# Attention's weight-by-value products: high and low halves in one 512-column product, with odd heads' values stored low half first

## The chip, the cores and the metric

The kernel runs on one core of a Trainium2 chip, as one launch. A core has five engines with instruction queues of their own: TensorE (PE; matrix products, its weight loads are shown as PEld), VectorE (DVE), ScalarE (ACT), GpSimd (POOL) and SyncE (SP, which here only issues transfers). The metric is device time in microseconds. Before the change the median of three runs is 2846.95 us (2845.26 to 2849.56).

## The reference

One decoder layer over 2048 tokens of 1024 features, in fp32: a token mixer (a depthwise convolution group beside a group of 8 attention heads of 64), cross attention into 256 memory tokens, and an MLP with squared ReLU, each with an RMS norm before and after. What matters here is the attention:

```
logits = einsum("bqhd,bkhd->bhqk", qb, kb) * scale
logits = logits + cum[:, :, q0:kl, None] - cum[:, :, None, :kl]   # forget-gate bias
p = softmax(where(mask, logits, NEG_INF))                         # causal
out = einsum("bhqk,bkhd->bqhd", p, vb)
```

## The kernel before

Features lie on partitions and tokens along the free axis; tokens are taken in 4 chunks of 512. TensorE multiplies `float32r` operands. To hold precision each fp32 operand is split into a high half (a ScalarE copy into `float32r`) and a low half (VectorE: the value minus its high half), and a product of two fp32 matrices is three products: high by high, high by low, low by high (`mm3`, lines 165 to 167).

**Attention's values.** `mix_in` projects 128 tokens by 4 heads at a time and stores for each head and token 128 numbers: its 64 high, then its 64 low halves (lines 365 to 370). So one 128x128 stationary tile holds both halves of V of one head for 128 keys: its output has 128 partitions, 64 from the high and 64 from the low half.

**Weight by value.** `values` (line 581) does it for one head and 256 queries (`QB`), in groups of two key tiles of 128. For each group TensorE transposes the softmax weights into the PSUM tile `pt` (line 595, three or four products of 128 columns), ScalarE and VectorE split `pt` into the two halves of `pp` (line 599), and, one group later, TensorE multiplies into the PSUM tile `o` (line 611): for each key tile one product of 256 columns by the high half of the weights and one by the low half, all added in the same 256 columns. The last key tile of a block meets only the second 128 queries, with products of 128 columns. When the block is done, `otmp` gathers the two partition halves of `o`: ScalarE copies one, VectorE adds the other (lines 617 and 618), and SP stores it to `datt`. `o` has one PSUM bank, `pp` two slots, and `otmp` shares the three slots of the tag `bs` with the diagonal bias `dg` (line 544), which GpSimd makes.

There are 64 such blocks: 8 heads, 4 chunks, 2 blocks of queries each. A block has 2, 4, ... 16 key tiles, by its place in the sequence.

**What sets the order.** A generator for the main stream (projections, then the MLP of an earlier chunk) and one for the side stream (attention, output projection, cross attention) are driven in step by the costs that they yield (`drive`); the convolution's taps are put between as background work for VectorE. The framework's scheduler then orders each engine's instructions by priorities counted in instructions (`ahead`, `steps`) and by when it holds them to be ready. From `attend(0)` on, the products of line 611 so stand between the main stream's `mm` products, in an order that is fixed before the launch.

Of the kernel before, what the change touches and what calls it, by code (L numbers as in the profile page):

```python
# [38 lines left out]
# Slots of the tile tags. Tiles of one tag are handed out in program order, so each stream of work  # L39
# (projections and MLP; attention and cross attention; convolution) has tags of its own.  # L40
BUFS = {
    "wr": 2, "wh": 2, "wl": 2, "xh": 1, "xl": 1,          # 4 KB: weights, raw and split
    "mk": 6, "bk": 7, "vk": 1,                            # 8 KB
    "mu": 5, "bu": 2, "bp": 2,                            # 4 KB
    "ms": 4, "bs": 3, "vs": 4,                         # 2 KB
    "row": 2,
    "mm": 2, "sc": 2, "pt": 2, "o": 1, "stat": 1,         # PSUM banks
# [3 lines left out]
# Chunk 0 takes also the slots that attention does not need then.  # L51
# [3 lines left out]
# The schedule: how far streams' instructions are put ahead of (h*), the work that they are given beside  # L55
# the main stream (r0, a1, m*), that of the convolution (a0, b1, bm), and what steps count for (y*).
# [4 lines left out]
class Engine:  # L61
    """An engine; pinned, it takes its instructions in program order."""
# [18 lines left out]
class Trunk:  # L81
# [13 lines left out]
    # ---------------------------------------------------------------- tiles  # L95
# [17 lines left out]
    # -------------------------------------------------------------- helpers  # L113
    @contextmanager
    def ahead(self, n):
        """Instructions put n places ahead of the others'."""
        n = 0 if Engine.pinned else n
        self.tc.cur_priority -= int(n)
        yield
        self.tc.cur_priority += int(n)  # L120
# [17 lines left out]
    def scaled_split(self, hi, lo, x, s):  # L138
        """(hi, lo) of x * s, s a constant or one value per partition."""
        self.a.activation(hi, x, AF.Copy, scale=s)  # L140
        self.v.scalar_tensor_tensor(
            out=lo, in0=x, scalar=s, in1=hi.bitcast(F32), op0=ALU.mult, op1=ALU.subtract)

    def weight(self, src, shape, into=None, g=MAIN):
        """One 4 KB per partition block of weights as float32r high and low parts."""
# [14 lines left out]
    def mm3(self, ps, lhs, rhs, first=True, last=True):  # L160
        """ps (+)= sum over k of lhsT.T @ rhs, each operand a (high, low) pair."""
# [15 lines left out]
    def token_mean(self, ss, mean):  # L177
        """Mean over the features of ss ([128, w], partial sums): PSUM [128, w / 128], tokens on partitions."""
# [6 lines left out]
    def token_rstd(self, ss, mean):  # L185
        """1 / sqrt(mean + eps) per token, as token_mean."""
# [6 lines left out]
    def spread(self, r):  # L193
        """Values per token, [128, n] with tokens on partitions -> PSUM [128, n * 128], the same on every partition."""
# [12 lines left out]
    def pair8(self, w, name, tags):  # L207
        """Two high and two low [128, 4, w] tiles, in the order h l h l of the tags."""
# [3 lines left out]
    # ------------------------------------------------------------ constants  # L212
# [51 lines left out]
    # ---------------------------------------------------- memory keys/values  # L264
# [13 lines left out]
    def normed(self, xs, g, w, stag, out=None, tags=None):  # L278
        """rms_norm of xs, two [128, 4, w] tiles, in place; with tags also split, as in halves."""
# [20 lines left out]
    def halves(self, out, xs, w, tags):  # L300
        """out: the float32r (high, low) tiles of xs, two [128, 4, w] tiles."""
# [34 lines left out]
    # ------------------------------------------------- token mixer, projection  # L336
    def mix_in(self, h, ht, late, after):
        """Input projection of half h; late brings its second chunk, after follows its first chunk's last use."""
# [16 lines left out]
        for b in range(2):  # L355
# [5 lines left out]
            for t in range(8):  # L361
# [3 lines left out]
                v = self.tile("ms", [P, 4, 2, DH], F32R, name="v")  # L365
                pv = ps[:, :256].rearrange("p (h d) -> p h d", d=DH)
                self.split(v[:, :, 0], v[:, :, 1], pv)
                self.store(
                    self.d_v[h][4 * b : 4 * b + 4, :, t].rearrange("h p d -> p h d"),
                    v.bitcast(F32).rearrange("p h l d -> p h (l d)"))  # L370
# [41 lines left out]
    def conv_push(self, c, t):  # L412
        """Background vector work: the depthwise convolution of channel tile t in chunk c, to DRAM."""
# [21 lines left out]
    def conv_norm(self, a, tag):  # L435
        """LayerNorm over the channels and swish of a ([128, 4, 512]), in place."""
# [22 lines left out]
    def gate(self, h, ht):  # L459
        """-cumsum(log_sigmoid(h @ w_f + b_forget)) of one half, to DRAM."""  # L460
# [31 lines left out]
    # ------------------------------------------------------ forgetting attention  # L492
    def attend(self, c):
        """Queries of chunk c against all keys up to them, head by head."""
# [86 lines left out]
    def values(self, c, hd, b, prow, v):  # L581
# [4 lines left out]
        o = self.ps("o")[:, :QB]  # L586
        prev = None
        for k0 in range(0, nk + 2, 2):
            cur = None
            if k0 < nk:  # L590
                # The last key tile meets only the second half of the queries.
# [9 lines left out]
            if prev is not None:  # L601
                g, pp = prev
                order = [(0, 0), (0, 1), (1, 0), (1, 1)]
                if g == nk - 2:
                    order = [(0, 0), (1, 0), (1, 1), (0, 1)] if g == 0 else order[2:] + order[:2]
                for n, (k, l) in enumerate(order):
                    if g + k == nk - 1:
                        out, rhs = o[:, P:], pp[:, l, QB : QB + P]
                    else:
                        out, rhs = o, pp[:, l, k * QB : (k + 1) * QB]  # L610
                    nc.tensor.matmul(out, v[:, g + k], rhs, start=g == 0 and n == 0, stop=g == nk - 2 and n == 3)  # L611
# [473 lines left out]
```

## Time and profile before

| | |
|---|---|
| time, median of 3 runs | 2846.95 us (2845.26 to 2849.56) |
| profiled execution: span from the first to the last instruction | 2843.6 us |
| median above that span (launch and end; the page has no other time) | 3.3 us |
| TensorE products busy | 2779.2 us, 98%, 14020 products |
| TensorE weight loads busy | 2310.6 us, 81% |
| VectorE busy | 1967.2 us, 69%, 3521 instructions |
| ScalarE busy | 1380.7 us, 49% |
| GpSimd busy | 206.5 us, 7% |
| products of line 611 | 1152 of the 14020 |

A product's busy time in the profile is its time from start to modelled end. Products are pipelined, so the next starts before that end: what a product costs in a stream is the distance from its start to the next one's start, its pitch. "Idle" of an engine is given with its releaser, the work that ended the wait.

### The profile page before, as it was taken

Reading aid. Unit: us, or ns where it says so; the run is one execution under the profiler, and the core shown is the slowest. Engines: PE = TensorE matmul, PEld = TensorE weight load, DVE = VectorE, ACT = ScalarE, POOL = GpSimd, SP = SyncE. Lnnn points to the kernel's source line nnn. Section 1 sums busy time; section 2 is a strip of 40 time slices with the busy share of each in tenths; the row PEclk is TensorE's granted clock in tenths of the full one; section 3 lists DMA queues with packets and bytes.
Section 4 is the critical chain, followed back from the end, with each engine's and each line's share of the span. In section 5 each row is a group of like instructions: output and inputs, shape, how many; then the busy total and the mean of one; then the engine's idle time right before and its main releaser. Section 6 shows DMA issues by size and latency. Waiting matters only on the chain.

```text
span 2843.6 us, 37412 instructions
## 1 busy us (share of the span) xinstructions
PE 2779.2 (98%) x14020; PEld 2310.6 (81%) x14020; DVE 1967.2 (69%) x3521; ACT 1380.7 (49%) x2164; POOL 206.5 (7%) x367
## 2 busy tenths in 40 slices
PE   7999999999999999999999999999999999999998
PEld 6889778888888887878888888788887888888887
DVE  7877896769787676788886645886665555743446
ACT  5323654345654445466554445665554445543332
POOL 0010300001110000012100001020100000000000
PEclk9999999999999999999999999999999999999999
DMA  5365744456544444455543435464524342343232
GB/s 168 117 217 170 174 128 163 141 164 200 154 137 132 124 136 145 149 151 175 138 142 119 146 108 166 129 197 129 155 94 128 126 145 93 130 144 97 96 97 81
DMA packets 141045, 398.32 MB, mean 140 GB/s; under 512 B 15248, under 2 KB 37904, under 8 KB 136000
## 3 DMA queue, kind: packets, MB, share of 16 engines
q1 hardware_dynamic: 99952, 262.40, 28.9%
q0 software_dynamic: 40912, 133.54, 16.4%
q8 instruction: 110, 1.80, 0.3%
q14 instruction: 71, 0.58, 0.1%
HBM read 330.68 MB, written 65.20 MB: 139 GB/s over the span
## 4 chain that ended last, share of the span: by engine, by line
PE 80%; issue 4%; DMA 4%; DVE 4%; ACT 2%; POOL 0%; SPq 0%; DVEq 0%; POOLq 0%; ACTq 0%
PE mm L165 18%; PE mm L166 18%; PE mm L167 18%; PE o L611 5%; PE sc L167 4%; PE sc L165 4%; PE sc L166 4%; PE pt L595 3%; PE sc L561 2%; PE sc L562 2%; DMA ks<-dk 1%; DVE acc L73 1%; DVE yacc L73 1%; DMA wr<-in_w_up_dram 1%; PE stat L182 1%
## 5 line engine op out<-in xcount | busy, mean ns | idle before, releaser
L73 ACT CAST wh<-wr 128x1024 fp32r<-128x1024 f32 x282 | 296.6, 1052 | 715.5 <-PE mm L166 634.1
L165 PE MATMUL mm<-h,wh 128*128 128x512 f32 x1504 | 597.6, 397 | 5.5 <-ACT h L73 2.6
L167 PE MATMUL mm<-h,wl 128*128 128x512 f32 x1504 | 596.9, 397 | 0.0
L166 PE MATMUL mm<-h,wh 128*128 128x512 f32 x1504 | 595.1, 396 | 1.7 <-DVE h L73 1.7
L73 DVE TENSOR_TENSOR wl<-wr,wh 128x1024 fp32r<-128x1024 f32 x282 | 345.5, 1225 | 277.2 <-ACT wh L73 276.0
L165 PE MATMUL mm<-hid,wh 128*128 128x512 f32 x992 | 395.3, 399 | 0.4 <-DVE yacc L73 0.4
L167 PE MATMUL mm<-hid,wl 128*128 128x512 f32 x992 | 392.8, 396 | 0.0
L166 PE MATMUL mm<-hid,wh 128*128 128x512 f32 x992 | 392.8, 396 | 0.0
L73 DVE SCALAR_TENSOR_TENSOR acc<-cu,convw,acc 128x512 f32<-128x512 f32 x480 | 356.9, 747 | 5.8
L165 PEld LDWEIGHTS mm<-h,wh 128*128 128x128 f32 x1504 | 283.9, 189 | 65.2 <-ACT h L73 2.9
L166 PEld LDWEIGHTS mm<-h,wh 128*128 128x128 f32 x1504 | 283.8, 189 | 60.1 <-DVE h L73 3.2
L167 PEld LDWEIGHTS mm<-h,wl 128*128 128x128 f32 x1504 | 283.6, 189 | 58.4
L73 DVE TENSOR_TENSOR yacc<-mm,yacc 128x512 f32<-128x512 f32 (+1 forms) x232 | 155.0, 669 | 160.3 <-PE mm L167 158.7
L73 DVE TENSOR_TENSOR pp<-pt,pp 128x512 fp32r<-128x512 f32 (+1 forms) x288 | 186.9, 656 | 68.0 <-ACT pp L73 66.6
L73 ACT CAST pp<-pt 128x512 fp32r<-128x512 f32 (+1 forms) x288 | 159.5, 560 | 124.6 <-PE pt L595 116.0
L165 PEld LDWEIGHTS mm<-hid,wh 128*128 128x128 f32 x992 | 186.3, 188 | 39.6 <-DVE yacc L73 1.5
L167 PEld LDWEIGHTS mm<-hid,wl 128*128 128x128 f32 x992 | 186.5, 188 | 38.5 <-issue 0.5
L166 PEld LDWEIGHTS mm<-hid,wh 128*128 128x128 f32 x992 | 186.6, 188 | 36.5 <-DVE hid L73 0.3
L595 PE MATMUL pt<-ident,prow 128*128 128x128 f32 x1088 | 199.3, 274 | 1.0 <-ACT prow L73 0.9
L73 ACT ACTIVATE prow<-prow,mx 128x128 f32<-128x128 f32 (+15 forms) x128 | 154.2, 1205 | 76.7 <-DVE mx L73 74.1
L73 DVE CUSTOM_DVE_ANT_0 prow<-sc,bias 128x512 f32<-128x512 f32 (+3 forms) x288 | 166.8, 596 | 34.3 <-PE sc L562 29.6
L611 PE MATMUL o<-pp,vv 128*128 128x256 f32 (+1 forms) x832 | 178.8, 299 | 8.6 <-DVE pp L73 7.9
(234 smaller groups left out, 4585.5 us busy)
## 6 DMA issues: line engine op xcount, KB each, us to landing
wr<-in_w_up_dram SPq DMA_DIRECT2D x128, 512.0 KB, 3.5
wr<-in_w_down_dram SPq DMA_DIRECT2D x128, 512.0 KB, 3.5
wr<-in_w_in_dram SPq DMA_DIRECT2D x32, 512.0 KB, 4.4
q<-dq POOLq DMA_DIRECT2D x64, 256.0 KB, 6.1
wr<-in_w_out_dram SPq DMA_DIRECT2D x32, 512.0 KB, 3.5
dx<-y SPq DMA_DIRECT2D x16, 1024.0 KB, 4.2
bias<-dnc POOLq DMA_DIRECT2D x32, 512.0 KB, 5.7
x<-in_x_dram POOLq DMA_DIRECT2D x12, 1024.0 KB, 5.9
```

The lines of the kernel that those rows point to most:

```text
L73: ins = op(*args, **kw)
L165: mm(ps, ah, bh, start=first and j == 0, stop=False)
L166: mm(ps, ah, bl, start=False, stop=False)
L167: mm(ps, al, bh, start=False, stop=last and j == n - 1)
L182: self.nc.tensor.matmul(ps[:, t : t + 1], ss[:, t * P : (t + 1) * P], mean, start=True, stop=True)
L561: nc.tensor.matmul(ps[:, :w], q[:, 0, qs], ks[:, k0 : k0 + w], start=True, stop=False)
L562: nc.tensor.matmul(ps[:, :w], q[:, 1, qs], ks[:, k0 : k0 + w], start=False, stop=True)
L595: nc.tensor.transpose(pt[:, at : at + P], prow[t][:, (k0 + k) * P : (k0 + k + 1) * P], self.ident)
L611: nc.tensor.matmul(out, v[:, g + k], rhs, start=g == 0 and n == 0, stop=g == nk - 2 and n == 3)
```

## The change

In `mix_in`, the tile `v` has four groups of 64 for each pair of heads: the even head's high and low, then the odd head's low and high. In `values`, one product takes both halves of the weights: its moving operand is two runs of 256 numbers, the high and the low half of `pp`, and its output is the whole bank of `o`, 512 columns. The stationary tile is the same. So the output has four quarters: (V high, V low) by (weights high, weights low). The last key tile takes two runs of 128. Three of the quarters are added at the end, V low by weights low is not taken: ScalarE copies the quarter from the other partitions, and VectorE adds two quarters from the head's own partitions, where the odd heads now have their high half too.

```diff
-                v = self.tile("ms", [P, 4, 2, DH], F32R, name="v")
-                pv = ps[:, :256].rearrange("p (h d) -> p h d", d=DH)
-                self.split(v[:, :, 0], v[:, :, 1], pv)
+                v = self.tile("ms", [P, 2, 4, DH], F32R, name="v")
+                pv = ps[:, :256].rearrange("p (g e d) -> p g e d", e=2, d=DH)
+                self.split(v[:, :, 0:4:3], v[:, :, 1:3], pv)
                 self.store(
                     self.d_v[h][4 * b : 4 * b + 4, :, t].rearrange("h p d -> p h d"),
-                    v.bitcast(F32).rearrange("p h l d -> p h (l d)"))
+                    v.bitcast(F32).rearrange("p g (e l) d -> p (g e) (l d)", e=2))
...
-        o = self.ps("o")[:, :QB]
+        o = self.ps("o").rearrange("p (l q) -> p l q", l=2)
...
-                order = [(0, 0), (0, 1), (1, 0), (1, 1)]
-                if g == nk - 2:
-                    order = [(0, 0), (1, 0), (1, 1), (0, 1)] if g == 0 else order[2:] + order[:2]
-                for n, (k, l) in enumerate(order):
-                    if g + k == nk - 1:
-                        out, rhs = o[:, P:], pp[:, l, QB : QB + P]
-                    else:
-                        out, rhs = o, pp[:, l, k * QB : (k + 1) * QB]
-                    nc.tensor.matmul(out, v[:, g + k], rhs, start=g == 0 and n == 0, stop=g == nk - 2 and n == 3)
+                every, late = slice(0, QB), slice(P, QB)
+                if g < nk - 2:
+                    order = [(0, every), (1, every)]
+                elif g > 0:
+                    order = [(1, late), (0, every)]
+                else:
+                    order = [(0, slice(0, P)), (0, late), (1, late)]
+                for n, (k, q) in enumerate(order):
+                    at = 0 if k == 0 else QB - q.start
+                    nc.tensor.matmul(o[:, :, q], v[:, g + k], pp[:, :, at + q.start : at + q.stop],
+                                     start=g == 0 and k == 0 and (n == 0 or nk == 2),
+                                     stop=g == nk - 2 and (n != 0 if g > 0 else n != 1))
...
-        self.a.copy(tmp[mine], o[other])
-        self.add(tmp[mine], o[mine], tmp[mine])
+        self.a.copy(tmp[mine], o[other, 0])
+        self.add(tmp[mine], o[mine, 0], tmp[mine])
+        self.add(tmp[mine], o[mine, 1], tmp[mine])
```

The rest of the diff takes out comments. On TensorE, the 1152 products of line 611 (1024 of 256 columns, 128 of 128) become 584 (504 of 512 columns, 80 of two runs of 128); the columns are 278,528 as before. VectorE gets 64 instructions more, the second add of each block. No transfer is added or changed in size.

The scheduler sets the order anew. TensorE, chunk 2, first head, its first block of queries; `o` is that block's sum, `pp` and `pt` a group's weights before and after the split, `mm` a product of the MLP. Before:

```order
L595 MATMUL pt_10598<-ident,prow_10443 128x128
L611 MATMUL o_10507<-pp_10591,vv_10427 128x256
L165 MATMUL mm_10652<-hid_10336,wh_10648 128x512
L166 MATMUL mm_10652<-hid_10336,wh_10648 128x512
L167 MATMUL mm_10652<-hid_10336,wl_10649 128x512
L165 MATMUL mm_10670<-hid_9983,wh_10648 128x512
L611 MATMUL o_10507<-pp_10591,vv_10427 128x256 x3
```

The same group after the change (line 595 is line 597 there, and 611 is 615):

```order
L597 MATMUL pt_10476<-ident,prow_10323 128x128
L166 MATMUL mm_10524<-hid_10216,wh_10520 128x512
L167 MATMUL mm_10524<-hid_10216,wl_10521 128x512
L165 MATMUL mm_10542<-hid_9863,wh_10520 128x512
L166 MATMUL mm_10542<-hid_9863,wh_10520 128x512
L615 MATMUL o_10387<-pp_10471,vv_10307 128x512 x2
```

One high-half product stood right behind the transposes and the other three behind four `mm` products; now both products stand behind the four.

VectorE at the end of the same block; `otmp` is the gathered output, `yacc`, `ssy` and `h` belong to the MLP and to the output projection. Before:

```order
L73 TENSOR_TENSOR yacc_6067<-yacc_6067,r2b_10378 128x512
L73 TENSOR_TENSOR otmp_10710<-o_10507,otmp_10710 64x256
L73 TENSOR_TENSOR yacc_6067<-yacc_6067,r2b_10378 128x512
L73 TENSOR_TENSOR ssy_10385<-ssy_10385,sq_10667 128x512
L73 SCALAR_TENSOR_TENSOR h_1703_10452<-y_1590_9795,gains,h_1702_10451 128x512 x2
```

After:

```order
L73 TENSOR_TENSOR otmp_10580<-o_10387,otmp_10580 64x256
L73 TENSOR_TENSOR yacc_6031<-yacc_6031,r2b_10258 128x512
L73 TENSOR_TENSOR ssy_10265<-ssy_10265,sq_10539 128x512
L73 TENSOR_TENSOR otmp_10580<-o_10387,otmp_10580 64x256
L73 SCALAR_TENSOR_TENSOR h_1703_10332<-y_1590_9675,gains,h_1702_10331 128x512
```

The second add stands two instructions of other work behind the first.

## Rows read from the trace of the kernel before

**Rows 1.** The page: span, and busy time, share and instructions of an engine.

```profile
span 2843.6 us, 37412 instructions
...
PE 2779.2 (98%) x14020; PEld 2310.6 (81%) x14020; DVE 1967.2 (69%) x3521; ACT 1380.7 (49%) x2164; POOL 206.5 (7%) x367
```

**Rows 2.** Windows: busy us (instructions) by engine, granted clock, DMA share, GB/s.

```profile
core 0: us, PE busy (x) PEld busy (x) DVE busy (x) ACT busy (x) POOL busy (x), PEclk, DMA share, GB/s
...
300.00:400.00 100.00, 94.99 (x498) 73.87 (x498) 87.98 (x235) 66.81 (x134) 25.42 (x46) 1.00 0.65 169
...
1200.00:1300.00 100.00, 94.16 (x496) 77.42 (x495) 89.19 (x204) 63.55 (x101) 17.87 (x32) 0.95 0.47 141
...
1800.00:1900.00 100.00, 93.94 (x542) 79.86 (x541) 89.20 (x205) 66.38 (x101) 15.39 (x28) 1.00 0.52 155
...
2600.00:2700.00 100.00, 100.00 (x443) 82.83 (x442) 42.51 (x48) 33.99 (x43) 0.00 (x0) 1.00 0.30 96
```

**Rows 3.** Timeline, 512-column products of the MLP: start, us, engine, line; first and last of 46.

```profile
2599.78 0.39 PE L165 MATMUL mm<-hid,wh 128*128 128x512 f32 x1
...
2609.98 0.39 PE L165 MATMUL mm<-hid,wh 128*128 128x512 f32 x1
```

**Rows 4.** Timeline, 256-column products of the value projection, first and last of 52.

```profile
251.77 0.28 PE L166 MATMUL mm<-wv,h 128*128 128x256 f32 x1
...
257.89 0.28 PE L166 MATMUL mm<-wv,h 128*128 128x256 f32 x1
```

**Rows 5.** Timeline, seven products of line 611 in a row, and the next product.

```profile
1333.01 0.98 PE L611 MATMUL o<-pp,vv 128*128 128x256 f32 x7
1333.83 0.40 PE L165 MATMUL mm<-hid,wh 128*128 128x512 f32 x1
```

**Rows 6.** Groups by form, line 611: count, busy us, mean ns, idle before, releasers.

```profile
L611 PE MATMUL o<-pp,vv 128*128 128x256 f32 x768 | 171.9, 303 | 8.2 <-DVE pp L73 7.4 <-ACT pp L73 0.6
...
L611 PE MATMUL o<-pp,kv 128*128 128x256 f32 x256 | 58.6, 301 | 1.8 <-DVE pp L73 0.6 <-ACT pp L73 0.5 <-DVE otmp L73 0.2
...
L611 PE MATMUL o<-pp,kv 128*128 128x128 f32 x64 | 15.1, 253 | 0.8 <-DVE mx L73 0.4 <-ACT pp L73 0.2
L611 PE MATMUL o<-pp,vv 128*128 128x128 f32 x64 | 14.9, 253 | 0.5 <-DVE pp L73 0.5
```

**Rows 7.** Groups on VectorE: the existing add of each block.

```profile
L73 DVE TENSOR_TENSOR otmp<-o,otmp 64x256 f32<-64x256 f32 x64 | 26.9, 421 | 15.0 <-ACT otmp L73 13.9
```

**Rows 8.** Windows, instructions of `otmp` alone: DVE busy (count), ACT busy (count).

```profile
300.00:400.00 100.00, 6.74 (x16) 5.88 (x16) 1.00 0.65 169
1200.00:1300.00 100.00, 1.69 (x4) 1.47 (x4) 0.95 0.47 141
1800.00:1900.00 100.00, 1.26 (x3) 1.10 (x3) 1.00 0.52 155
```

**Rows 9.** Waits, whole span: total us, times, longest.

```profile
POOL dg L544 <- DMA datt<-otmp: 77.9, 12, 11.3
...
PEld o L611 <- DVE pp L73: 20.4, 46, 3.1
...
PEld o L611 <- ACT pp L73: 15.4, 47, 0.9
...
PE o L611 <- DVE pp L73: 8.6, 8, 2.9
...
PE sc L561 <- DMA ks<-dk: 4.6, 5, 1.7
```

**Rows 10.** Timeline of TensorE, in chunk 2's attention: a product that waited.

```profile
1277.82 0.63 PE L611 MATMUL o<-pp,vv 128*128 128x256 f32 x3 [2.52 <-DVE pp L73]
```

**Rows 11.** Timeline of VectorE, the same place.

```profile
1275.82 0.69 DVE L73 TENSOR_TENSOR yacc<-yacc,x2r 128x512 f32<-128x512 f32 x1 [2.67 <-DMA x2r<-dx]
```

**Rows 12.** Window behind an earlier such wait, columns as in rows 2.

```profile
1240.00:1250.00 10.00, 8.65 (x36) 7.38 (x36) 8.62 (x22) 5.00 (x8) 0.00 (x0) 0.66 0.16 52
```

## The prediction

> **What bounds the kernel now.** I read the page's busy shares first: TensorE's products cover 98% of the span, VectorE 69%, ScalarE 49% [rows 1]. A busy share of products says little by itself, because each record holds a tail that overlaps the next product, so the second view was the windows by 100 us: in the late MLP TensorE is busy without a break at the full granted clock and VectorE is at 43%, while in three stretches of the attention VectorE stands at 88 to 89% and TensorE falls to 94 or 95% [rows 2]. Third, pitches from the timeline. 45 steps of 512-column products take 2609.98 - 2599.78 = 10.20 us, 0.2267 us each [rows 3]; 51 steps of 256 columns take 6.12 us, 0.120 us each [rows 4]. Two 256s so cost 0.240 against 0.227 for one 512: about 13 ns go with each product whatever its width. TensorE's stream of products is the bound, with VectorE close behind it in the attention. The waits named on line 611 are small: 8.6 us of product idle on VectorE's `pp`, and 20.4 and 15.4 us that weight loads waited for the low and the high half, part of it beneath a running product [rows 9].
>
> **TensorE: fewer, wider products.** Before, line 611 issues 768 + 256 = 1024 products of 256 columns and 64 + 64 = 128 of 128 [rows 6]. A stretch of seven of them, three of one group and the four of a block's last group (five of 256 columns, two of 128), takes 1333.83 - 1333.01 = 0.82 us to the next product [rows 5]. With 5 x 0.120 that leaves 0.22 for the two narrow ones, 0.110 each: a product of 128 columns is hardly cheaper than one of 256. So before costs 1024 x 0.120 + 128 x 0.110 = 122.9 + 14.1 = 137.0 us. After, 504 of 512 columns and 80 of 2 x 128 cost 504 x 0.2267 + 80 x 0.120 = 114.3 + 9.6 = 123.9 us. The difference is 13.1 us. The columns are the same on both sides; all of it is what 568 products cost beside their columns. The weight loads beside them go too, 568 of 14020, but they lie under products and are in the pitches already.
>
> What the trace has no row for is a moving operand of two runs (2 x 256 numbers, 2 KB apart) or an output of two runs (the 80). From the best side it costs what one run of the same width does, 0.227 and 0.120. From the other, as much as the two products that it replaces, 0.240 and 0.220: 504 x 0.240 + 80 x 0.220 = 138.6 us, 1.6 us more than before. I take the single-run pitch, since each run is hundreds of numbers long and the nearest rows show columns to be what is paid for; the other end is kept.
>
> [...]
>
> **The wait for the low half.** Before, a group's first product needed the high half alone; now the first needs both. Priced from the waits: the 54 on VectorE (46 and 8 times [rows 9]) would each have 0.107 us more behind them, one 512 in place of one 256, or 5.8 us. At best it is nothing. I take 0: in the new order both products stand behind the four `mm` products that stood between the halves before, so what covers the low half's arrival is still there, and the `mm` products themselves are only moved. If that cover falls short, each failing group holds up the following `mm` products and the scores with it.
>
> **VectorE: 64 more adds.** The add that is there takes 0.421 us on the mean [rows 7], and the second has the same form: 64 x 0.421 = 26.9 us. VectorE is idle in 31% of the span, which hides most. Where it is 88 to 89% busy there is little room: 16 + 4 + 3 = 23 blocks end there [rows 8], 23 x 0.421 = 9.7 us. Even there 11 to 12 us of each 100 are idle, and the convolution's taps can slip; at best all is hidden, at worst all 26.9 us reach TensorE. I take a third of the 9.7, 3.2 us. Behind an add on VectorE are the next splits of weights and `pp`, for which TensorE waits. The bank of `o` is held 0.42 us or more longer, and the next block's first product is queued behind its own transposes and split, so I cost that at 0; with that cover gone it would be another 64 x 0.42 us, the same time as the adds and not beside them. The store of `otmp` leaves as much later, and `dg` waits for its slot 12 times [rows 9] at the head of POOL's queue, with loads of K, V and bias behind it: 12 x 0.42 = 5.1 us at worst; TensorE waited for such a load 5 times, 4.6 us, so I take 0. At best here too nothing is lost.
>
> `mix_in`: 32 splits write another layout with as many numbers, and the transfers have the same size; 0. If these forms ran slower, the MLP-like pitch of that stage, whose VectorE has room, would cover it.
>
> **The order.** Because priorities count instructions, every stall in the attention falls elsewhere. The trace shows what one is: a load for the MLP's output lands late, VectorE stands 2.67 us behind it in order [rows 11], and TensorE 2.52 us behind VectorE [rows 10]. [...] Such accidents may go or come; a handful either way, 8 us on both sides, centre 0.
>
> **Sum.** Against the profiled span of 2843.6 us [rows 1]: 2843.6 - 13.1 + 3.2 = 2833.7. The median of the runs stands 3.3 us above that span (launch and end), so the time is 2837 us, 0.35% less.
>
> **Rivals.**
> Slower: VectorE decides. If the adds stand in the open, each pushes back the split for which TensorE waits. From 13.1 / 0.421 = 31 open adds of the 64 on, nothing is gained; all 64 give 2846.95 - 13.1 + 26.9 = 2860.8 us. For it speak the 88 to 89% of three stretches; against it that only 23 blocks end in them, and that VectorE is idle a third of the time.
> No change: the products get shorter where VectorE sets the pace. Then TensorE's waits on `pp` grow by what it saves. If half of the 13.1 is lost in this way and the 3.2 us stay, the time is 2846.95 - 6.5 + 3.2 = 2843.6 us. For it speak the waits on `pp` in both halves; against it that `mm` products fill in and that they are shortened by nothing.
> No change: two runs cost as two products, and the edit does not do what it says. 2846.95 + 1.6 + 3.2 = 2851.8 us by the upper price, and without the adds 2848.5. [...]
> [...]
>
> **How the numbers follow.** A measurement of this kernel can tell some 0.2%, 5.7 us, from no change. My forecast, about 2829 to 2841 us, has 0.70. Gain lost to waits 0.12; two runs as dear as two products 0.04; columns alone 0.02; VectorE (or a bad turn of the order beside it) 0.12. So faster 0.70, no change 0.18, slower 0.12. Low end: 2837 with the adds hidden (-3) and 8 us of stalls gone is 2826. High end: it takes in all of the cases of no change and a little of the slower one, with 2846.95 + 5.7 = 2852.7, so 2853.
>
> **What would show it.** Products of line 615 should start 0.227 us apart where they stand in pairs, and 584 of them be there; clearly more, 0.24 or above, is the two-run rival. VectorE's `otmp` group should hold 128 adds near 0.42 us. The windows of the attention, summed, should be some 10 us shorter, the late MLP the same. If VectorE's share there rises past 90% and PE's waits on `pp` or `mx` grow by over 10 us, VectorE has decided. If the attention is shorter and time is lost in waits on loads (`ks`, `x2r`) or at the lower clock, it is the order. I am wrong if the time is above 2841 us, and wrong in kind if the pitch of the wide products is not that of the MLP's.

## The result and the profile after

The changed kernel takes 2866.82 us (median of 4 runs, 2865.09 to 2872.11). One run of the kernel before stands at 11531.5 us and is left aside; the median of its other three is 2846.95 us. The ratio on record is 1.0075, with a 95% interval of 1.0062 to 1.0087, which is 21 us (18 to 25); the two medians lie 19.9 us apart. The kernel became slower; the forecast was 2837 us, faster.

The page of the changed kernel, span and busy time, share and instructions of each engine; the answer to it is [rows 1]:

```profile
span 2870.3 us, 36361 instructions
...
PE 2782.1 (97%) x13452; PEld 2283.8 (80%) x13452; DVE 1991.0 (69%) x3585; ACT 1379.6 (48%) x2164; POOL 207.9 (7%) x367
```

568 products are gone and 64 VectorE instructions have come, as the diff says, but the span is 26.7 us longer. That is more than the medians' 19.9 us, because the profiled execution after took 2872.11 us, 5.3 above its median, and the span before fits the run of 2845.26 us, 1.7 below its median. What follows accounts for these two executions.

First the products themselves. TensorE's timeline of the changed kernel (start, us, engine, line), a block's last four products and the next product:

```profile
1383.05 0.96 PE L615 MATMUL o<-pp,vv 128*128 128x512 f32 x4
1383.85 0.40 PE L165 MATMUL mm<-h,wh 128*128 128x512 f32 x1
```

The four take 0.80 us: three of 512 columns and the one of two runs of 128, 3 x 0.2267 + 0.120 = 0.80. Here a moving operand and an output of two runs cost what one run of the same width does [rows 3, 4]. By form, line 615 of the changed kernel (count | busy us, mean ns | idle before, and its releasers), the answer to [rows 6]:

```profile
L615 PE MATMUL o<-pp,vv 128*128 128x512 f32 x384 | 135.8, 415 | 11.0 <-DVE pp L73 10.8
...
L615 PE MATMUL o<-pp,kv 128*128 128x512 f32 x120 | 42.8, 412 | 2.5 <-DVE pp L73 2.5
...
L615 PE MATMUL o<-pp,kv 128*128 128x256 f32 x48 | 11.8, 301 | 0.1
L615 PE MATMUL o<-pp,vv 128*128 128x256 f32 x32 | 9.5, 298 | 0.0
```

These are 504 and 80 products. With the counts of all products and pitches of 0.227, 0.172, 0.1195 and 0.110 us for 512, 384, 256 and at most 128 columns (from [rows 3 to 5], and for 384 from two products into `sc` of before that start at 1825.96 and 1826.13 us), an estimate of TensorE's stream without a gap is 2713.1 us before and 2700.6 after. Only the difference is used: 12.5 us less, near the 13.1 of the prediction. So about 39 us must have come in elsewhere.

Windows of the changed kernel. The first, third, fourth and last row answer to [rows 2]:

```profile
core 0: us, PE busy (x) PEld busy (x) DVE busy (x) ACT busy (x) POOL busy (x), PEclk, DMA share, GB/s
300.00:400.00 100.00, 91.10 (x444) 70.92 (x443) 81.63 (x237) 58.97 (x126) 26.24 (x46) 0.97 0.64 169
400.00:450.00 50.00, 42.24 (x170) 31.93 (x169) 43.28 (x44) 20.28 (x23) 0.00 (x0) 0.97 0.19 60
...
1200.00:1300.00 100.00, 93.30 (x449) 75.19 (x448) 91.75 (x192) 62.63 (x98) 15.80 (x27) 0.97 0.51 150
...
1800.00:1900.00 100.00, 96.93 (x483) 79.19 (x482) 84.55 (x187) 65.09 (x97) 13.24 (x23) 0.98 0.45 145
1900.00:2000.00 100.00, 93.31 (x462) 74.13 (x462) 63.35 (x154) 54.68 (x84) 13.87 (x25) 0.97 0.53 160
2600.00:2700.00 100.00, 100.00 (x443) 82.84 (x442) 41.09 (x45) 38.44 (x52) 0.00 (x0) 1.00 0.29 95
```

Two of these stretches in the kernel before:

```profile
400.00:450.00 50.00, 49.38 (x214) 39.26 (x213) 35.54 (x35) 15.39 (x21) 0.00 (x0) 1.00 0.32 96
...
1900.00:2000.00 100.00, 99.66 (x574) 83.54 (x572) 64.14 (x162) 61.35 (x95) 14.24 (x27) 1.00 0.49 144
```

The late MLP is as it was. What was a stream without gaps at the full clock at 400 to 450 and 1900 to 2000 us now has gaps of 7 to 8 us and a clock of 0.97 (not quite the same work: the changed kernel is behind by then). The granted clock over the whole span, before and after:

```profile
core 0: 2843.6 us, clock 0.996
```

```profile
core 0: 2870.3 us, clock 0.989
```

By these shares, an estimate of the time lost to the lower clock is 0.004 x 2843.6 = 11.4 us before and 0.011 x 2870.3 = 31.6 us after.

The waits of TensorE's products (total us, times, longest), changed kernel, the first of 30 rows:

```profile
PE o L615 <- DVE pp L73: 13.3, 9, 3.7
PE stat L182 <- DVE nss L73: 12.2, 1, 12.2
PE sc L562 <- DMA ks<-dk: 7.8, 5, 2.4
PE sc L562 <- DVE mx L73: 7.3, 11, 1.8
PE sc L165 <- ACT xh L73: 4.1, 3, 2.3
PE stat L182 <- DVE ssy L73: 3.6, 1, 3.6
PE sc L166 <- DVE cat L73: 3.5, 1, 3.5
```

Of these, `o` on `pp` and `sc` on `ks` answer to [rows 9] (8.6 and 4.6). In the kernel before, two others were:

```profile
PE sc L561 <- DVE mx L73: 2.8, 4, 1.0
...
PE sc L165 <- ACT xh L73: 2.4, 2, 1.5
```

The rows of this view sum to 54.2 us before (31 rows) and 78.3 us after (30): 24.1 us more. 16.0 of them are at products into `sc`, the attention's scores and the output projection (14.7 to 30.7); products into `o` hold only 2.6 (10.7 to 13.3). So the account of the profiled spans is -12.5 (pitches), +24.1 (waits) and a rest of 15.1, for which 20.2 us more of lost clock are there, part of it inside the waits.

Where the time went can be read from products that both kernels have. Before: a product behind the split of `v`, ahead of the first attention blocks (timeline); the first product behind chunk 0's last block, on the row sums `rs`; and the first of chunk 0's cross attention, on `mk` (count, duration in ns, first and last start in us):

```profile
288.27 0.50 PE L165 MATMUL mm<-h,wh 128*128 128x512 f32 x1 [0.51 <-DVE v L73]
...
L535 PE MATMUL stat<-ident,rs x4: 270/271/273, 364.5 to 2138.5; 128*32 128x128 f32 x4
...
L165 PE MATMUL sc<-mk,mq x64: 277/280/388, 557.0 to 2360.4; 128*128 128x256 f32 x64
```

The same three after:

```profile
289.55 0.50 PE L165 MATMUL mm<-h,wh 128*128 128x512 f32 x1 [0.25 <-DVE v L73]
...
L536 PE MATMUL stat<-ident,rs x4: 270/272/284, 375.3 to 2161.0; 128*32 128x128 f32 x4
...
L165 PE MATMUL sc<-mk,mq x64: 274/280/386, 572.3 to 2386.8; 128*128 128x256 f32 x64
```

The changed kernel is behind by 1.3 us at the first, by 10.8 at the second and by 15.3 at the third; the other 11.4 of the 26.7 us come in the 2290 us that follow. So more than half is lost around chunk 0's attention. There 16 of the 64 second adds stand close together; the instructions on `otmp` alone (DVE and ACT busy), the answer to the first of [rows 8]:

```profile
300.00:400.00 100.00, 13.44 (x32) 5.87 (x16) 0.97 0.64 169
```

One piece can be followed by name. VectorE's timeline around the reciprocal of the attention's forget gate (second half of the tokens), before:

```profile
389.38 2.28 DVE L73 TENSOR_TENSOR cat<-cu,cat 128x2048 fp32r<-128x2048 f32 x1
...
392.19 2.27 DVE L73 TENSOR_TENSOR cat<-at,cat 128x2048 fp32r<-128x2048 f32 x1
...
399.08 6.53 DVE L73 RECIPROCAL gate<-gate 8x1024 f32<-8x1024 f32 x1
```

After, the reciprocal is ahead of the splits, though neither belongs to the change:

```profile
407.57 6.53 DVE L73 RECIPROCAL gate<-gate 8x1024 f32<-8x1024 f32 x1
414.04 2.22 DVE L73 TENSOR_TENSOR cat<-cu,cat 128x2048 fp32r<-128x2048 f32 x1
```

And TensorE, changed kernel, in the same place:

```profile
416.31 0.50 PE L166 MATMUL sc<-cat,xh 128*128 128x512 f32 x1 [3.51 <-DVE cat L73]
```

The output projection waits 3.51 us for a split that stands behind 6.53 us of other work on VectorE. What put the reciprocal ahead is not shown. Changed counts alone did not: of the kernels below, the changed one with the old counts has it ahead as well (401.6 us, the split 408.1), the one before with the new counts does not (399.5, the split 389.6).

The second piece is the kind of stall that [rows 10, 11] show. VectorE of the changed kernel:

```profile
1292.29 0.69 DVE L73 TENSOR_TENSOR yacc<-yacc,x2r 128x512 f32<-128x512 f32 x1 [4.02 <-DMA x2r<-dx]
```

and TensorE:

```profile
1289.59 0.40 PE L166 MATMUL mm<-h,wh 128*128 128x512 f32 x1
1293.73 1.04 PE L615 MATMUL o<-pp,vv 128*128 128x512 f32 x2 [3.75 <-DVE pp L73]
...
1296.28 0.63 PE L167 MATMUL mm<-h,wl 128*128 128x512 f32 x1
1296.71 0.63 PE L165 MATMUL mm<-h,wh 128*128 128x512 f32 x1
1297.14 0.48 PE L166 MATMUL mm<-h,wh 128*128 128x512 f32 x1
1297.45 0.39 PE L167 MATMUL mm<-h,wl 128*128 128x512 f32 x1
```

VectorE stands 4.02 us for the late load `x2r`, the split of `pp` next in its order starts at 1292.90 us, and TensorE stands 3.75 us. Then products of 512 columns start 0.43 us apart (1296.28, 1296.71, 1297.14) in place of 0.227; the granted clock there is 0.50, and 1.00 from 1297.50 us on:

```profile
1296.00:1297.10 1.10, 1.10 (x4) 0.85 (x3) 1.10 (x3) 1.10 (x2) 0.00 (x0) 0.50 0.81 142
```

The wait's row names `pp`; what was late is the load. This is no new stop but a longer one (2.52 us of TensorE before): VectorE's waits on `x2r` sum to 7.5 us before and 9.7 after.

### The profile page after: what moved, and what is told of

It reads as the page before. It is cut to its first block, busy times and chain, and to the rows that moved or that the text cites. A ratio compares the mean times of both kernels' runs of the same rounds, so it can differ in the third digit from the quotient of the medians.

```text
span 2870.3 us, 36361 instructions
## 1 busy us (share of the span) xinstructions
PE 2782.1 (97%) x13452; PEld 2283.8 (80%) x13452; DVE 1991.0 (69%) x3585; ACT 1379.6 (48%) x2164; POOL 207.9 (7%) x367
## 4 chain that ended last, share of the span: by engine, by line
PE 77%; issue 5%; DMA 5%; DVE 5%; ACT 1%; POOL 1%; DVEq 0%; POOLq 0%; ACTq 0%; SPq 0%
PE mm L165 17%; PE mm L166 17%; PE mm L167 17%; PE sc L167 4%; PE sc L165 4%; PE sc L166 4%; PE o L615 4%; PE pt L597 3%; PE sc L562 2%; PE sc L563 2%; DMA bias<-dnc 1%; DMA ks<-dk 1%; DMA cu<-du 1%; DVE yacc L73 1%; DVE acc L73 1%
## 5 line engine op out<-in xcount | busy, mean ns | idle before, releaser
L597 PEld LDWEIGHTS pt<-ident,prow 128*128 128x128 f32 x1088 | 142.2, 142 | 33.5 <-ACT prow L73 4.6
```

What stands on the lines that cost most here:

```text
L597: nc.tensor.transpose(pt[:, at : at + P], prow[t][:, (k0 + k) * P : (k0 + k + 1) * P], self.ident)
```

## The experiments

Three readings were set against each other. The adds: 64 more VectorE instructions reach TensorE. The low half: each group now waits for both halves. The order: any change of the instruction counts moves all work, and the order of before is one that the change loses. Each ratio is to the unchanged kernel on the same chip (medians there 2844.9 to 2847.9 us), with a 95% interval; 0.001 is 2.85 us.

**The add without the products.** The kernel before with a second VectorE instruction of the same form behind the add (maximum in place of sum, so the gathered output is not the reference's):

```diff
         self.add(tmp[mine], o[mine], tmp[mine])
+        self.v.tensor_tensor(out=tmp[mine], in0=o[mine], in1=tmp[mine], op=ALU.max)
```

> The kernel before, with a second VectorE instruction of the same size per block behind the add of otmp (64 more, a maximum of the same operands instead of the second quarter's sum, so the attention output is not the reference's). Theory V (the 64 adds stand in TensorE's way): slower, 2863 to 2875 us, with the after kernel's extra waits on pp and mx. Theory W (the product now waits for both halves): 2846 to 2850 us, as before. Theory O (the adds and waits are small in themselves, the new order of all engines loses time, because the schedule's distances are counted in instructions): a change of a few us, 2845 to 2860, with stalls in places that have nothing to do with the adds.

Measured 2870.2 us, 1.0089 [1.0064, 1.0113]: as slow as the whole change, with none of its products. Its waits of TensorE:

```profile
PE sc L561 <- DVE mx L73: 13.1, 10, 4.2
...
PE o L611 <- DVE pp L73: 4.9, 5, 1.7
```

The waits at `o` went down (8.6 in [rows 9]) and those of the scores on `mx`, their maxima on VectorE, rose from 2.8 to 13.1 us. What the instruction costs falls on other work of VectorE. Chunk 0's attention ends at 377.3 us here (364.5 before, by the same product as above), and the cross attention begins at 572.7 (557.0): 15.7 of the 21.7 us by which this profiled span is longer are lost by then.

**The products without the add.** The changed kernel, one quarter left out of the sum:

```diff
         self.add(tmp[mine], o[mine, 0], tmp[mine])
-        self.add(tmp[mine], o[mine, 1], tmp[mine])
```

> The kernel after, without the second add (the quarter V high by weights low is left out of the sum). V: the loss goes, 2834 to 2842 us. W: 2863 to 2868 us, as after. O: it stays slower than before, 2850 to 2868 us, since the order is still another.

Measured 2847.7 us, 1.0010 [1.0000, 1.0020]. Without the adds the loss is gone, and so is the one around chunk 0: its attention ends at 364.8 us and the cross attention begins at 558.4. But the 12.5 us that the pitches save are not seen either: the waits sum to 66.5 us against 54.2.

**The counts.** The changed kernel with the scheduler's counter moved as before the change, and the kernel before with it moved as after:

```diff
+                self.tc.cur_priority += 4 - len(order)     # changed kernel, each group
...
+        self.tc.cur_priority -= 1                          # behind the second add
```

> The kernel after, with the priorities counted as before: each group of products counts 4 places whatever it issues, and the second add counts none. The work is that of after. O: most of the loss goes, 2834 to 2850 us. V and W: 2863 to 2870 us, as after.

```diff
+                self.tc.cur_priority -= 1 if nk == 2 else 2     # kernel before, each group
...
+        self.tc.cur_priority += 1                               # behind the add
```

> The kernel before, with the priorities counted as after: each group of four products counts 2 places, the end of a block one more. The work is that of before, no instruction is added. O: slower by 8 to 25 us, 2856 to 2873. V and W: 2846 to 2850 us, as before.

Measured 2856.6 us, 1.0042 [1.0027, 1.0057], and 2849.6 us, 1.0013 [1.0001, 1.0024]. The old counts take 9 us off the changed kernel; the new counts put 4 us on the one before. So the counts alone are not all of it: the same counter doesn't give the same order where the instructions differ.

**The low half first.** The kernel before with the products by the low halves ahead of those by the high halves:

```diff
-                order = [(0, 0), (0, 1), (1, 0), (1, 1)]
+                order = [(0, 1), (0, 0), (1, 1), (1, 0)]
...
-                    order = [(0, 0), (1, 0), (1, 1), (0, 1)] if g == 0 else order[2:] + order[:2]
+                    order = [(0, 1), (1, 1), (1, 0), (0, 0)] if g == 0 else order[2:] + order[:2]
```

> The kernel before, with the low half's product ahead of the high half's in each pair, so that a group can't start until both halves are there, as after; widths, counts and adds are those of before. Theory W (the wait for both halves costs the 13 us by which the attention's idle time rose even without the second adds): slower by 8 to 16 us than before, 2853 to 2861. Theory V (the adds are all) and theory O (only a new order loses): within 5 us of before, 2841 to 2850; by O of either sign.

Measured 2855.8 us, 1.0033 [1.0023, 1.0044]. Its wait at `o`:

```profile
PE o L611 <- DVE pp L73: 17.0, 10, 5.3
```

To need the low half first costs 9 us here, and the wait that the reading names rose by 8.4 (8.6 to 17.0). In the changed kernel the same wait rose by 4.7 (8.6 to 13.3), inside the bound of 5.8. But order alone moves it as far: in the kernel before under the four other settings of the last experiment it is 1.4 to 12.0 us, in the changed kernel under the same settings 7.4 to 10.6. The 17.0 lies above that range, so needing the low half first can cost, though this edit too brought an order of its own. What of the 4.7 us in the changed kernel belongs to the low half is not shown.

**What of the add costs.** Three edits of the kernel before or after: an independent VectorE instruction of that size on a scratch tile; a second read of `o`, on ScalarE and not on VectorE (both on before; the second leaves one half out of the output); and, on the changed kernel, the second quarter copied out by ScalarE, its add and the store placed 40 places later.

```diff
+        self.scr = ct([P, QB], "scr")
+        self.v.memset(self.scr, 0.0)
...
+        self.v.tensor_tensor(out=self.scr[mine], in0=self.scr[mine], in1=self.scr[mine], op=ALU.max)
```

> The kernel before, with 64 more VectorE instructions of the size of the add, at the same place in the program, on a scratch tile that nothing else reads. If VectorE's time is what the added instruction costs: as e1_add_only, 2863 to 2872 us. If it is the chain (the bank of o and the slot of otmp held longer, the store later): 2843 to 2852 us.

```diff
+        self.a.copy(tmp[mine], o[mine])
```

> The kernel before, with a ScalarE copy of o into otmp behind the add, 0.37 us, so that the bank of o, the slot of otmp and the store are held as by a second add, but VectorE has no more to do (the attention output is then not the reference's, one partition half is left out). If the chain is the cost: 2860 to 2872 us. If VectorE's time is: 2842 to 2852 us.

```diff
-    "row": 2,
+    "row": 2, "bt": 1,
...
+        part = self.tile("bt", [P, QB], name="opart")
         self.a.copy(tmp[mine], o[other, 0])
+        self.a.copy(part[mine], o[mine, 1])
         self.add(tmp[mine], o[mine, 0], tmp[mine])
-        self.add(tmp[mine], o[mine, 1], tmp[mine])
-        self.store(self.d_att[c][hd // 2, mine, b * QB : (b + 1) * QB], tmp[mine])
+        with self.ahead(-40):
+            self.add(tmp[mine], tmp[mine], part[mine])
+            self.store(self.d_att[c][hd // 2, mine, b * QB : (b + 1) * QB], tmp[mine])
```

> The kernel after, with the third quarter copied out of PSUM by ScalarE at once (64 copies more, 0.37 us each) and the second add and the store put 40 places back, so that the bank of o is free sooner and VectorE isn't held at the block's end; VectorE's instructions are as many as in after. If the add's place is what costs: 2846 to 2854 us, towards e2_no_second_add. If VectorE's time or a new order costs: 2858 to 2870 us.

Measured 2853.5 us, 1.0026 [1.0015, 1.0037]; 2849.6 us, 1.0011 [0.9997, 1.0024]; 2857.2 us, 1.0042 [1.0028, 1.0056]. The scratch instructions in their kernel, as a group (busy us, mean ns) and by the time of the first and the last start:

```profile
L73 DVE TENSOR_TENSOR scr<-scr 64x256 f32<-64x256 f32 x64 | 26.6, 415 | 1.4
...
L73 DVE TENSOR_TENSOR scr<-scr x64: 353/420/424, 1.6 to 125.9; 64x256 f32<-64x256 f32 x64
```

They did not run at the blocks' ends. Nothing holds them there, and the scheduler put all 64 into the first 126 us, long before the attention. That stretch, in this kernel and in the one before:

```profile
0.00:126.00 126.00, 103.43 (x460) 82.59 (x461) 122.53 (x202) 56.86 (x78) 5.64 (x14) 0.99 0.41 132
...
0.00:126.00 126.00, 108.06 (x492) 86.75 (x493) 106.78 (x147) 58.81 (x81) 5.48 (x14) 1.00 0.45 143
```

VectorE is busy for 122.53 us in place of 106.78, and the first split of `v` starts at 249.9 us in place of 243.7. So the 7.4 us are the price of 26.6 us of VectorE work at the start of the program; of the add in its place this run says nothing. The longer hold of `o` by ScalarE costs 3.1 us [-0.9, 6.8], not told from nothing: the bank is not the main matter. Moving the add out of the way gives back 9 of 21 us; it does not bring the kernel under the one before.

**The add, with the counter held.**

```diff
+        self.v.tensor_tensor(out=tmp[mine], in0=o[mine], in1=tmp[mine], op=ALU.max)
+        self.tc.cur_priority -= 1
```

> The kernel before with the second VectorE instruction of e1_add_only (a maximum instead of the quarter's sum, so the attention output is not the reference's), but not counted in the priorities. Theory V (the add in its place costs 25 us in itself): 2865 to 2874 us, as e1_add_only. Theory O (most of those 25 us came with the order that the 64 extra places made; the add's own price is the 7 us of e6_free_add plus some for the chain): 2850 to 2860 us.

and the changed kernel without the second add, with the old counts of its groups:

```diff
+                self.tc.cur_priority += 4 - len(order)
...
-        self.add(tmp[mine], o[mine, 1], tmp[mine])
```

> The kernel after without the second add (one quarter left out of the sum) and with priorities counted as before: products of 512 columns alone. By the sum of pitches, 12.5 us under before: 2830 to 2836 us. If the wait for both halves costs what the products save: 2843 to 2849 us, as e2_no_second_add. If the count was what e2_no_second_add lost: 2830 to 2838.

Measured 2866.8 us, 1.0070 [1.0055, 1.0085], and 2850.3 us, 1.0007 [0.9993, 1.0020]. The counter is not what makes the added instruction dear: held, it costs 20 us in place of 25, and the two intervals overlap. But its sequence on the engines is a new one in each of these kernels, so this doesn't separate the instruction from the order.

**The same instructions in other orders.** If the order of before is a good one among many, the kernel before must lose when only its order is moved, and the changed kernel need not. One number of the schedule decides how far attention's instructions are put ahead of the others (`hs`), another how far the main stream's are (`hm`). Each was set alone, with not an instruction more or less.

```diff
-SCHED = dict(hw=135, hb=117, hs=62.8, hm=39.2, ...
+SCHED = dict(hw=135, hb=117, hs=58.8, hm=39.2, ...
```

and so for `hs` 66.8 and 54.8, and for `hm` 35.2. First the kernel before, `hs` 58.8 and 66.8:

> The kernel before with one number of the schedule changed, the side stream 58 places ahead instead of 62: the same instructions in another order. How much an order alone is worth. Theory O: 4 to 15 us slower, 2850 to 2862. Theory V and W: within 3 us of before.

> The kernel before with the side stream 66 places ahead instead of 62, the same instructions in another order. Theory O: 4 to 15 us slower, 2850 to 2862, by an amount unlike that of e11_ahead_58. Theory V and W: within 3 us of before.

then the changed kernel with the same two:

> The kernel after with the side stream 58 places ahead, as e11_ahead_58 is of before (2853 us). Theory O alone (the work of after is 12.5 us less TensorE time, all else is order): anywhere from 2838 to 2862 us, on either side of e11_ahead_58, and not near 2867 again. Theory X (the added waits and adds cost 25 to 30 us in any order): slower than e11_ahead_58 by 10 to 20 us, 2863 to 2873.

> The kernel after with the side stream 66 places ahead, as e12_ahead_66 is of before (2868.6 us). O alone: 2838 to 2866 us, below e12_ahead_66. X: above e12_ahead_66 by 10 to 20 us, 2878 to 2888.

and both with `hs` 54.8 and with `hm` 35.2:

> The kernel after with the side stream 54 places ahead, a fourth order. O alone: 2838 to 2862 us. X: 2860 to 2880.

> The kernel before with the side stream 54 places ahead, the pair of a3_ahead_54 (2850.4 us). Theory O (the order is worth up to 20 us, the change's own effect is a gain of some us): 2846 to 2872 us, more likely above a3_ahead_54 than below. Theory X (the changed instructions cost 10 us or more in any order): at least 10 us under a3_ahead_54, 2840 or less.

> The kernel after with the main stream 35 places ahead instead of 39, a fifth order. O alone: 2838 to 2862 us. X: 2860 to 2880.

> The kernel before with the main stream 35 places ahead, the pair of a4_main_35 (2857.5 us). O: 2846 to 2872 us, more likely above 2857 than below. X: 2847 or less.

Measured (ratio to the kernel before as given). The last three columns are read from one profiled run of each, before and changed: the waits of products, those into `sc`, and the end of chunk 0's attention, by the first product on `rs`. The profiled run of the changed kernel at `hs` 58.8 lies 10.6 us above its median.

| setting | before, us | ratio | changed, us | ratio | waits, us | into `sc` | `rs`, us |
|---|---|---|---|---|---|---|---|
| as given | 2846.95 | 1 | 2866.82 | 1.0075 [1.0062, 1.0087] | 54.2, 78.3 | 14.7, 30.7 | 364.5, 375.3 |
| `hs` 58.8 | 2853.1 | 1.0024 [1.0012, 1.0036] | 2848.6 | 1.0013 [1.0001, 1.0025] | 59.1, 74.5 | 16.7, 26.6 | 367.2, 369.3 |
| `hs` 66.8 | 2868.6 | 1.0072 [1.0054, 1.0091] | 2854.4 | 1.0027 [1.0015, 1.0039] | 64.9, 69.4 | 20.6, 27.9 | 363.0, 370.2 |
| `hs` 54.8 | 2852.0 | 1.0019 [1.0002, 1.0035] | 2850.4 | 1.0016 [1.0005, 1.0026] | 57.5, 68.3 | 14.1, 21.0 | 363.1, 368.8 |
| `hm` 35.2 | 2863.7 | 1.0062 [1.0046, 1.0078] | 2857.5 | 1.0033 [1.0017, 1.0049] | 60.2, 70.9 | 14.7, 29.0 | 363.3, 373.2 |

The kernel before, none of its instructions changed, loses 5 to 21 us by its order alone. With `hs` 66.8 it is as slow as the changed kernel. In four of five settings the changed kernel is the lower of the two (by 0.0003 to 0.0045, clearly so at `hs` 66.8); in the given one alone it is the higher. The given order is the best of five for the kernel before and the worst of five for the changed one. The means over the five are 1.0035 and 1.0033. Their difference is under 1 us, but five pairs so scattered leave it open by 16 us either way (95%), so the gain of 10 us that was forecast lies inside. Without the given setting the mean of the four differences is 6 us in favour of the change, open by 8.5.

Two things hold in every pair. The changed kernel has more waits than the other, by 4.5 to 24.1 us, mean 13.1, above all into `sc`: about what the pitches save. And its chunk 0 attention ends later, by 2.1 to 10.8 us, mean 7.1; the 16 second adds there are 16 x 0.42 = 6.7 us of VectorE. No version ran faster than the kernel before.

## Why the prediction was wrong

**Right.** The products: 584 of them, at the pitch of one run, 12.5 us less by the counts and pitches where 13.1 were forecast. With that two rivals fall. By the rows at 1383.05, two runs as dear as two products would make those four 3 x 0.240 + 0.220 = 0.94 us, where 0.80 stands. Columns alone, at 0.02, has two products of 256 cost what one of 512 does: they cost 0.240 us and it costs 0.2267 [rows 3, 4], in the changed kernel too by those four. One step was too wide: the 13 ns "whatever its width" come from 256 and 512 columns alone, by which 128 columns would take 0.067 us, where [rows 5] leave 0.110. Also right: the second add's own size, in the changed kernel (the answer to [rows 7])

```profile
L73 DVE TENSOR_TENSOR otmp<-o,otmp 64x256 f32<-64x256 f32 x128 | 53.7, 420 | 27.5 <-ACT otmp L73 25.6
```

128 at 0.420 us; and the late MLP, which didn't move.

**The first step that failed: "The order".** "Such accidents may go or come; a handful either way, 8 us on both sides, centre 0." The mechanism was named, and the size and the sign were wrong. The kernel before, moved in its order and in nothing else, lost 5 to 21 us in four of four tries; its counter moved, 4 us in a fifth. No try gained. The order of before is on the good side of those tried, so a move away from it had a centre of some 10 us (mean of 6.8, 20.5, 5.4, 17.6 and 3.7 us: 10.8), not 0. No run shows the 8 us, which were my estimate of such stops. By the granted clock in windows of 0.5 us, an estimate of what a clock below 1.00 took is 1.7 us at the stop of 3.75 us in the changed kernel (0.50 from 1294.0 to 1297.0 us) and 3.4 us in the window of [rows 12] (0.50 from 1242.0 to 1248.5 us). The rows of before had a sign of the size of the order: the waits of TensorE's products alone sum to 54.2 us, and 8 us are 15% of that. The wait in the window of [rows 12] is also of another kind than [rows 10, 11]: 1.30 us of waiting for `pp`, up to 1242.53 us, with no late load on VectorE near it.

**The second: "VectorE: 64 more adds".** Taken at 3.2 us within 0 to 26.9. In place, with against without it, the ratios differ by 10 us (old counts), 18.5 (the change as it is), 20 and 25 us (the kernel before, counter held or not). All lie inside the bounds and all are above what I took. The prediction saw the tight place, the 23 blocks that end where VectorE is 88 to 89% busy, and charged a third of their adds. For 16 of them, chunk 0's, take the time from the product behind the split of `v` to the end of the attention. With the add it is 8.6 us longer than without it in the changed kernel (289.55 to 375.3 against 287.64 to 364.8) and 13.1 us longer in the kernel before (287.93 to 377.3 against 288.27 to 364.5): more than the whole length of those adds, 6.7 us. How much of the rest is the add and how much the order that came with it stays open.

**The wait for the low half.** Taken at 0 with 5.8 as the bound. The wait on `pp` rose by 4.7 us in the changed kernel; in the kernel before with the low half first it rose by 8.4. Order alone moved it from 1.4 to 12.0, so the 0 is neither shown nor refuted.

Booked one by one, the given case is: products alone +3 us against before, although their pitches say -12.5; the second add +18.5 on top; together 21. That is one booking of several, since each step brings an order of its own; in this one the adds are the larger miss, and the order ate what the products saved. The 3.3 us from span to time do not matter, but are not launch and end alone: the runs on record stand 1.7 to 2.1 us above their spans.

**The rivals.** That VectorE decides had the right sign and 0.12, and its 2860.8 us lies 6 us under the result. Of its signs, VectorE's share rose past 90% in one of the three windows (91.75) and fell in the two others (81.63 and 84.55, for 87.98 and 89.20 in [rows 2]); the waits of `o` on `pp` and of `sc` on `mx` rose by 4.7 and 4.5 us, together just under the 10 that I had set. So these signs did not decide; the ends of chunk 0's attention speak for this rival in that stretch. The sign that I had set for the order, time lost in waits on `ks` or `x2r` or at the lower clock, came in part: `ks` 4.6 to 7.8 us, `x2r` on VectorE 7.5 to 9.7, 20 us more of lost clock. But its other half, a shorter attention, did not. "Gain lost to waits" is the nearest to what the five orders show, though not at its 2843.6 us and not by waits on `pp` alone: the waits grow in all of them.

**What is settled and what is not.** Shown: the products run at the pitch of one run, which by the counts is 12.5 us less; the order of the same instructions is worth 5 to 21 us; in the given order the change loses 21 us, nearly all of which goes with the second add; more than half of the loss in the profiled runs falls around chunk 0's attention. That the given order suited the kernel before and not the changed one is the luck of this pair, or the outcome of settling constants such as 62.8 on the kernel before; the record does not say which. Not settled: what the change is worth in a typical order (a gain of 10 us and a loss of 10 both fit), and how the 21 us divide between the adds and the order. The reciprocal stands ahead of the `cat` splits in all five orders of the changed kernel and in the kernel before at `hs` 58.8, and behind them in its other four. The six with it ahead begin chunk 0's cross attention at 560.6 to 572.3 us, the four others at 555.7 to 557.0. So it may weigh some us, though it doesn't make the given order the worst; to move it alone was not tried, nor to move the add in chunk 0 alone.

## What to carry to other kernels

Where a static order was settled for one set of instructions, price any edit that changes them with the loss of that order, and measure what an order is worth: move one number of the schedule, with no other edit, on both kernels. A saving below that spread (5 to 21 us here, for a saving of 12.5) can't be judged from one order; compare the two kernels over several. Compare the start times of products that both kernels have at a few places: they tell where the time was lost before any theory does. Price an added instruction at its full length or more where its engine is nearly full: here 6.7 us of adds came with 8.6 and 13.1 us, where VectorE stood at 87.98%. And look up where an added instruction ran before reading its price.

## What the runs showed of the hardware that was not expected

A moving operand of two runs of 256 numbers, 2 KB apart, and an output of two runs of 128 cost a product nothing here (0.80 us for the four at 1383.05). Behind one stop of TensorE, the 3.75 us that follow the product at 1289.59, the products of 512 columns ran 0.43 us apart at a granted clock of 0.50; from 1297.45 us on they were 0.23 apart again. No kind of wait of TensorE's products differs by more than 4.7 us between the two kernels, and yet 15.3 of the 26.7 us were lost by the start of chunk 0's cross attention: the list of waits shows no one place, the times of common products do. 64 scratch instructions of 0.415 us, which nothing waits for, cost 7.4 us where VectorE was already busy for 106.78 of 126 us.
